# Rotary query stores, one gating piece and one cumulative sum moved to other places in a two-branch attention block

## The chip, the core and the metric

The kernel runs on one core of one Trainium2 chip. The core has five engines that work at the same time: TensorE (PE, matrix products into PSUM), VectorE (DVE), ScalarE (ACT), GpSimd (POOL) and SyncE (SP, which here only issues DMA transfers; the 16 DMA engines of the core move the data). The metric is the device time of one execution in microseconds (us), smaller being better; several executions are timed and their median is taken.

## The reference

The program is one layer of a decoder block: two attention branches side by side, latent attention with a rotary part (MLA, called branch 0 in the kernel) and attention with a forget gate (FoX, branch 1), 16 heads each, 512 real positions after 16 leading ones, width 1024, everything in float32. Cut to what matters:

```python
u = rmsnorm(h, pre_norm_g)
(cq, ckv, k_pe_raw, z_mla, fq, fk, fv, f_logit, z_fox, gate_a, gate_b) = split(u @ w_in)
q = rmsnorm(cq) @ w_uq                  # 16 heads of 64 + 32 (the 32 are rotary)
kv = rmsnorm(ckv) @ w_ukv               # 16 heads of 64 keys + 64 values
k_pe = rope(k_pe_raw, pos);  q_m = [q_nope, rope(q_pe, pos)];  k_m = [k_nope, k_pe]
o_mla = softmax(causal(q_m k_m^T * scale)) v_mla
cum = cumsum(log_sigmoid(f_logit + fox_forget_b))
o_fox = softmax(causal(fq fk^T * scale + cum[t] - cum[s])) fv
y_mla = (o_mla * silu(z_mla)) @ w_br_mla;   y_fox = (o_fox * silu(z_fox)) @ w_br_fox
mixed = (sigmoid(gate_a) * y_mla + sigmoid(gate_b) * y_fox) @ w_out
out = (h + rmsnorm(mixed, post_norm_g))[n_meta:]
```

## The kernel before

**Precision.** Each float32 factor of a product is split into a high part (rounded to the format that PE multiplies fast) and a low part (the rest), and a product is three matmuls: high x high, high x low, low x high. So each weight tile needs, after its load from HBM (`wraw`), a cast on ACT (`wh`, L127) and a subtraction on POOL (`wl`, L102) before PE can use it; the third matmul of each group of three is the first to read `wl`. Three `wraw`, `wh` and `wl` buffers go round.

**Units and fills.** The work of PE is cut into units: `fq`, `fk`, `v` (FoX queries, keys, values of a pair of heads), `mq`, `mk`, `v` (the same of MLA), `z` (the inputs of the silu, one tile of each branch), `pg` (the two gates) and `ppe` (the rotary queries of eight heads). A unit is a list of steps; a step is three matmuls over one block of 128 of the inner dimension, and the first step of a unit asks for its weights and starts the loads of the next three units. `unit`, `weights`, `wsplit` and `run` (which calls a list of steps) do this.

**Stages.** After a first part (norms, the latent projections, the first FoX queries and keys) come 16 stages, one for each pair of heads and branch, FoX and MLA by turns: stage 0 is FoX pair 0, stage 1 is MLA pair 0, stage 2 FoX pair 1, and so on. A stage is: `s0`, the scores of query blocks 0 to 2 (`st` on PE, three bank pairs of 144 + 272 and 400 columns); the value products `ov` of the stage before (`late`, `va`); `s1`, the scores of block 3; and then a fill, the units that the next stage needs, with the gates spread over some stages. Each run of scores is masked on DVE with the row extreme (`sf`, L761), exponentiated on ACT (L769), normalised and split on ACT and DVE (`pn`, L796 and L797) and transposed by eight DMA transpositions on SP (`pt<-pn`, L802). The values are transposed in the same way (`vp<-vh`, L700). `ov` needs both. The score tiles have four PSUM banks, so `s1` can begin only when DVE has read the first banks of `s0`; the units share three PSUM banks (`accp`).

**The order.** PE's order is written out by hand (a manual schedule: PE runs what the program text lists, in that order). The other engines are ordered by a scheduler that goes through the program by readiness and priority; three things tie it: `tc.high_priority`, `tc.issue_after(ins)` (what is written in the block is queued behind `ins`, if it is on the same engine) and `tc.keep_in_program_order` (queued behind what was written last on that engine). `written[0] = True` makes the helper `dma` (L90) do the last for every transfer. `behind` is a list of instructions behind which `wsplit` queues its ACT cast. Each engine then runs its own list strictly in order, so an instruction that waits holds all that follows on that engine. In the built program, transfers take one of eight completion semaphores in turn, whichever engine issues them, and the issuing engine waits until the transfer that had that semaphore before has landed.

**The places that the change touches.**

- `hl_done` (L232): the evacuation of queries and keys, a copy on ACT (L241, kept in `halved`) and the low part on DVE (L242). The keys come in two halves of 272 and 256 columns.
- L504 to L528: the first FoX queries and keys (`qk`), between them the log forget gates: `Abs`, `Exp`, `Ln` on ACT, L513 and the running sum `tensor_tensor_scan` (L514) on DVE, then `ch` (L519 on ACT, L521 on DVE), which goes out by DMA to `CT` and `c_dram`. `run(qk[7:])` holds all steps of the first keys.
- `pe_unit` (L593): the rotary queries. `rest` (L631) turns them on POOL and puts the result into `gT0` and `gT1`; those of pair 0 go to `QP` directly (L645), those of pairs 1 to 7 go by `store` (L647) to `qpe_dram` in HBM, four transfers of 192 KB, and are read back as `QP<-qpe_dram` one pair at a time, first for stage 3.
- `first` (L846): the rotary unit, the first FoX values, and the first four of the eight steps of gate unit `pg00`. The other four (`begun`) open the fill of stage 0.
- the stage loop (L880). In stage 0, `s0` and `s1` run back to back, then `fill[:5]` (four gating steps and one `z` step), the transposition of the FoX values, the `QP` transfers, both normalisations, and the rest of the fill: `z` of FoX, `mq`, `z` of MLA with `mk` and `v` in between. After it the four stores are written with `nc.scalar.dma_start`, so they are issued by ACT's queue, the first two behind the copy of `mq`, the other two behind the second copy of `mk`.

## Time and profile before

| | us |
|---|---|
| median of three timed executions (614.07 to 617.99) | 615.04 |
| the profiled execution | 616.33 |
| its span, from the first to the last instruction on the core | 614.5 |
| what lies around the span | 1.83 |
| PE busy | 600.5 (98%) |
| ACT, DVE, POOL busy | 329.9, 311.5, 264.1 |

The mean granted PE clock was 0.996 of full speed. The profile has one page of totals (busy time of each engine, the span in 40 slices, the DMA queues, the chain of waits that ended last, the costliest groups of instructions) and views into the trace: a timeline of an engine in a window (start, duration, engine, line, operation, what it writes and reads, and in brackets the idle time ahead of it and what ended it), the chain of waits in order of time, and tables of windows. In the tables of windows a row is the window, its length, the busy time of PE, PEld (weight loads), DVE, ACT and POOL with the number of instructions, the granted PE clock, the mean share of the 16 DMA engines and GB/s. SPq and ACTq are the queues from which SP and ACT issue transfers; the duration of such a row is the issuing, not the transfer. Matmuls overlap, so the time that one costs is the distance to the start of the next.

### The profile page before, as it was taken

Reading aid. Unit: us, or ns where it says so; the run is one execution under the profiler, and the core shown is the slowest. Engines: PE = TensorE matmul, PEld = TensorE weight load, DVE = VectorE, ACT = ScalarE, POOL = GpSimd, SP = SyncE. Lnnn points to the kernel's source line nnn. Section 1 sums busy time; section 2 is a strip of 40 time slices with the busy share of each in tenths; the row PEclk is TensorE's granted clock in tenths of the full one; section 3 lists DMA queues with packets and bytes.
Section 4 is the critical chain, followed back from the end, with each engine's and each line's share of the span. In section 5 each row is a group of like instructions: output and inputs, shape, how many; then the busy total and the mean of one; then the engine's idle time right before and its main releaser. Section 6 shows DMA issues by size and latency. Waiting matters only on the chain.

```text
span 614.5 us, 11031 instructions
## 1 busy us (share of the span) xinstructions
PE 600.5 (98%) x3821; PEld 508.9 (83%) x3821; DVE 311.5 (51%) x925; ACT 329.9 (54%) x758; POOL 264.1 (43%) x266
## 2 busy tenths in 40 slices
PE   7999989999999999999999999999999999999996
PEld 6888768889889889888898898878888888888885
DVE  4946637665775765675656657717222022024034
ACT  7846727765774775675667657737222232232321
POOL 4317506453437544353533534452544444444610
PEclk9999989999999999999999999999999999999999
DMA  9434487979688687997688786771523333224602
GB/s 299 102 81 127 94 173 134 226 169 206 125 178 177 153 192 161 188 185 186 145 144 179 171 176 151 175 159 36 157 84 101 103 102 97 89 91 126 251 35 102
DMA packets 223704, 89.59 MB, mean 146 GB/s; under 512 B 141772, under 2 KB 216916, under 8 KB 223648
## 3 DMA queue, kind: packets, MB, share of 16 engines
q1 hardware_dynamic: 223240, 88.09, 60.6%
q10 hardware_dynamic: 408, 0.79, 0.5%
q8 instruction: 30, 0.49, 0.3%
q14 instruction: 26, 0.21, 0.1%
HBM read 54.43 MB, written 4.00 MB: 95 GB/s over the span
## 4 chain that ended last, share of the span: by engine, by line
PE 85%; ACT 4%; DVE 4%; issue 3%; DMA 2%; POOL 1%; SPq 0%; ACTq 0%; DVEq 0%; POOLq 0%
PE py L96 14%; PE z L96 14%; PE pg L96 14%; PE po L96 7%; PE fk L96 7%; PE v L96 7%; PE fq L96 6%; PE st L96 6%; PE ov L96 4%; DVE sf L761 2%; PE psm L96 2%; PE mq L96 2%; DMA pt<-pn 1%; ACT uTh L373 1%; PE mk L96 1%
## 5 line engine op out<-in xcount | busy, mean ns | idle before, releaser
L102 POOL TENSOR_TENSOR wl<-wraw,wh 128x1024 fp32r<-128x1024 f32 (+1 forms) x90 | 208.0, 2315 | 208.4 <-ACT wh L127 202.3
L127 ACT CAST wh<-wraw 128x1024 fp32r<-128x1024 f32 (+1 forms) x90 | 89.9, 1003 | 163.6 <-issue 46.8
L769 ACT ACTIVATE sf<-sf,nb 128x144 f32<-128x144 f32 (+3 forms) x128 | 72.1, 565 | 13.8 <-DVE nb L761 13.8
L797 DVE SCALAR_TENSOR_TENSOR pn<-sf,ri,pn 128x128 f16<-128x128 f32 (+3 forms) x128 | 68.7, 575 | 13.2 <-ACT pn L796 13.1
L796 ACT ACTIVATE pn<-sf,ri 128x128 f16<-128x128 f32 (+3 forms) x128 | 61.5, 551 | 19.9 <-ACT sf L769 17.9
L957 DVE SCALAR_TENSOR_TENSOR tb<-th,py 128x512 f32<-128x512 f32 x16 | 11.0, 688 | 101.9 <-PE py L96 101.9
L96 PE MATMUL st<-hlk,hlq 64*128 64x272 f32 (+3 forms) x480 | 50.9, 310 | 1.2 <-DVE nb L761 0.6
L96 PE MATMUL z<-uTh,wh 128*128 128x512 f32 x128 | 50.8, 397 | 0.0
L761 DVE CUSTOM_DVE_ANT_0 sf<-st,maskt 128x272 f32<-128x272 f32 (+2 forms) x128 | 48.4, 435 | 3.8 <-PE st L96 2.9
L96 PE MATMUL pg<-uTh,wh 128*128 128x512 f32 x128 | 50.2, 392 | 0.0
L96 PE MATMUL z<-uTh,wl 128*128 128x512 f32 x128 | 50.0, 391 | 0.0
L96 PE MATMUL z<-uTl,wh 128*128 128x512 f32 x128 | 49.9, 390 | 0.0
L96 PE MATMUL pg<-uTl,wh 128*128 128x512 f32 x128 | 49.8, 389 | 0.0
L96 PE MATMUL pg<-uTh,wl 128*128 128x512 f32 x128 | 49.8, 389 | 0.0
L96 PE MATMUL py<-gh,wh 128*128 128x512 f32 x128 | 49.8, 389 | 0.0
L96 PE MATMUL py<-gl,wh 128*128 128x512 f32 x128 | 49.8, 389 | 0.0
L96 PE MATMUL py<-gh,wl 128*128 128x512 f32 x128 | 49.8, 389 | 0.0
L783 POOL TENSOR_TENSOR mt<-sf,ri 128x96 f32<-128x96 f32 (+1 forms) x32 | 9.5, 295 | 83.1 <-DVE ri L778 71.7
L96 PEld LDWEIGHTS st<-hlk,hlq 64*128 64x128 f32 x480 | 36.9, 185 | 8.9 <-DVE nb L761 3.4
L96 PE MATMUL ov<-pt,vp 128*64 128x256 f16 (+4 forms) x416 | 35.1, 317 | 2.7 <-DMA qpe_dram<-gT 2.7
L96 PE MATMUL v<-uTh,wh 128*128 128x256 f32 (+1 forms) x128 | 36.7, 287 | 0.6 <-DVE hlk L102 0.4
L96 PEld LDWEIGHTS <-vp 128*64 128x64 f16 (+1 forms) x416 | 22.9, 113 | 16.6 <-issue 5.3
(191 smaller groups left out, 1416.5 us busy)
## 6 DMA issues: line engine op xcount, KB each, us to landing
wraw<-in_w_in_dram SPq DMA_DIRECT2D x56, 512.0 KB, 4.7
wraw<-in_w_br_fox_dram SPq DMA_DIRECT2D x8, 512.0 KB, 3.5
wraw<-in_w_br_mla_dram SPq DMA_DIRECT2D x8, 512.0 KB, 3.8
wraw<-in_w_out_dram SPq DMA_DIRECT2D x8, 512.0 KB
pt<-pn SPq DMA_TRANSPOSE x128, 2.6
xr<-in_x_dram SPq DMA_DIRECT2D x4, 512.0 KB
out_dram<-yo SPq DMA_DIRECT2D x8, 256.0 KB, 2.0
QP<-qpe_dram SPq DMA_DIRECT2D x7, 256.0 KB, 2.8
```

Of the source, the lines that this page charges most:

```text
L96: nc.tensor.matmul(*a, **k)
L102: return eng.tensor_tensor(out=lo, in0=src, in1=f32(hi), op=ALU.subtract)
L127: nc.scalar.copy(wh[:, :n], raw[:, :n])
L373: pin(nc.scalar.activation(hi, src, AF.Copy, scale=gk))
L761: nc.vector.tensor_tensor_reduce(out=sf_of(h, b)[:, c0 : c0 + w], in0=ps[h][:, o : o + w], in1=maskt[:, m0 : m0 + w], scale=-scale, scalar ...
L769: exps[g] = nc.scalar.activation(sf, sf, AF.Exp, bias=sums["nb"][:, h, b : b + 1], scale=-1.0, accum_out=sums["su"][:, h, b : b + 1]).ins
L783: nc.gpsimd.tensor_tensor(out=mt, in0=src, in1=ri.unsqueeze(3).broadcast_to([128, 2, nb_, META]), op=ALU.mult)
L796: nc.scalar.activation(hi, sf, AF.Copy, scale=rib)
L797: nc.vector.scalar_tensor_tensor(out=lo, in0=sf, scalar=rib, in1=hi, op0=ALU.mult, op1=ALU.subtract)
L957: nc.vector.scalar_tensor_tensor(out=tb[br], in0=ths[i, br], scalar=1.0, in1=py, op0=ALU.add, op1=ALU.mult)
```

## The change

Three edits, with no change to what is computed, and with the same instructions and transfers in number:

- **The stores.** The four stores of the rotary queries are no longer written at the end of stage 0 with ACT as the issuing engine. They are written in stage 1, after its `s1` and ahead of its fill, whose first step is the transposition of the MLA values (`vp<-vh`, "second values"). SP issues them, and each is queued behind what was written last on SP.
- **The gating piece.** In stage 0, three of the four remaining steps of `pg00` (nine matmuls of 512 columns) run between `s0` and `s1` instead of after `s1`. The other stages keep their order.
- **The first keys.** The running sum on DVE is now queued behind the low part of the second half of the first keys. The ACT cast of the weights of `pg00` is queued behind the copy of that half.

```diff
-    behind, through, first_t, exps, halved = [], [], [], [], {}
+    behind, through, first_t, exps, halved, lowered = [], [], [], [], {}, {}
...
-                split_lo(nc.vector, hl[:, 1, o : o + w_], ps, hl[:, 0, o : o + w_])
+                lowered[key, i] = split_lo(nc.vector, hl[:, 1, o : o + w_], ps, hl[:, 0, o : o + w_]).ins
...
-        nc.vector.tensor_tensor_scan(out=fa[:, 0], data0=fa[:, 1], data1=fa[:, 2], initial=0.0, op0=ALU.add,
-                                     op1=ALU.add)
         run(qk[7:])
+        with tc.issue_after(lowered[("k", 1, 0), 1]):
+            nc.vector.tensor_tensor_scan(out=fa[:, 0], data0=fa[:, 1], data1=fa[:, 2], initial=0.0, op0=ALU.add,
+                                         op1=ALU.add)
...
-            def store(x, a, b, start=None):
+            def store(x, a, b):
                 for i in range(2):
-                    dma(qpe_dram[8 * g + a : 8 * g + b, i, x], results(x)[16 * a : 16 * b, i], start)
+                    dma(qpe_dram[8 * g + a : 8 * g + b, i, x], results(x)[16 * a : 16 * b, i])
...
-        run(first[len(pe0) :])
+        run(first[len(pe0) : -4])
+        behind[:] = [halved[("k", 1, 0), 1]]
+        run(first[-4:])
+        behind.clear()
...
-            for fn in [s0] + late + [s1]:
+            fill = fills[si]
+            for fn in [s0] + late:
                 fn()
-
-            fill = fills[si]
             if si == 0:
-
-                run(fill[:5])
+                run(fill[:3])
+            s1()
+
+            if si == 0:
+
+                run(fill[3:5])
                 run(vts[1, 0] + pe_rest)
                 n0()
                 n1()
                 first_t.extend(through)
                 run(fill[5:])
-                written[0] = False
-                for x in range(2):
-                    with tc.issue_after((halved[("q", 0, 0), 0], halved[("k", 0, 0), 1])[x]):
-                        store0(x, 2, 8, nc.scalar.dma_start)
-                written[0] = True
             else:
-                run(fill[:1])
-                run(fill[1:5])
+                if si == 1:
+
+                    written[0] = True
+                    for x in range(2):
+                        store0(x, 2, 8)
+                    written[0] = False
+                run(fill[:5])
```

## The prediction, made before the changed kernel was run

> **What bounds the kernel now.** The page came first: PE is busy for 600.5 of 614.5 us, so the time is PE's work and the few places where PE stands still or is slow. The table of windows says where those are.

> ```profile
> 82.00:94.00 12.00, 8.85 (x79) 6.35 (x78) 4.00 (x18) 5.33 (x16) 2.59 (x2) 0.86 0.86 174
> 94.00:200.00 106.00, 105.80 (x806) 92.32 (x807) 69.85 (x221) 68.17 (x162) 52.44 (x67) 1.00 0.83 173
> ```

> From 94 us on PE hardly stops. Between 82 and 94 us, where stage 1 begins, 3.15 us are idle and the clock was lowered (0.86 in the mean). The timeline of PE for this stretch, and for stage 3, which is the same MLA stage one pair later:

> ```profile
> 82.27 0.56 PE L96 MATMUL st<-hlk,hlq 64*128 64x144 f32 x6
> ...
> 84.56 0.40 PE L96 MATMUL ov<-pt,vp 80*64 80x512 f16 x1
> 87.62 3.61 PE L96 MATMUL ov<-pt,vp 80*64 80x512 f16 x25 [2.66 <-DMA qpe_dram<-gT]
> 91.43 0.39 PE L96 MATMUL st<-hlk,hlq 64*128 64x272 f32 x1 [0.20 <-DVE nb L761]
> ...
> 93.79 0.50 PE L96 MATMUL fq<-uTh,wh 128*128 128x512 f32 x1
> ```
> ```profile
> 130.56 0.56 PE L96 MATMUL st<-hlk,hlq 64*128 64x144 f32 x6
> ...
> 132.86 2.04 PE L96 MATMUL ov<-pt,vp 80*64 80x512 f16 x26
> ...
> 136.68 0.50 PE L96 MATMUL fq<-uTh,wh 128*128 128x512 f32 x1
> ```

> From the first score to the first `fq` stage 3 takes 136.68 - 130.56 = 6.12 us, stage 1 takes 93.79 - 82.27 = 11.52 us, with the same instructions. The 5.40 us between them are three things: `ov` waits from 84.96 to 87.62; its other 25 matmuls take 3.61 us where stage 3 needs 2.04 for 26; and the second score run then waits for DVE (`nb`). What `ov` waits for is seen in the chain of waits, on ACT's queue and on SP's:

> ```profile
> 78.41 9.12 DMA pt<-pn
> ...
> 87.61 0.71 ACTq L90
> ```
> ```profile
> 75.66 2.10 ACTq L90 DMA_DIRECT2D qpe_dram<-gT  x2
> ...
> 80.67 7.65 ACTq L90 DMA_DIRECT2D qpe_dram<-gT  x2
> 88.37 0.29 ACT L687 ACTIVATE vh<-v,vsc 128x32 f16<-128x32 f32 x1 [9.11 <-DMA pt<-pn]
> ```
> ```profile
> 68.39 13.32 SPq L90 DMA_TRANSPOSE pt<-pn  x8
> 81.77 2.32 SPq L90 DMA_DIRECT2D wraw<-in_w_in_dram  x2
> 84.18 2.62 SPq L90 DMA_DIRECT2D CT<-c_dram  x2
> 90.82 1.27 SPq L90 DMA_TRANSPOSE vp<-vh  x1
> ```
> ```profile
> pt<-pn SPq DMA_TRANSPOSE x128, 2.6
> ```

> The last of stage 0's eight transpositions is issued at 78.41 and lands at 87.53, 9.12 us later, against a median of 2.6. In just that time the stores of the rotary queries are in flight. ACT issues the fourth store at 87.61, as soon as that transposition has landed: it holds the completion semaphore that the store is to have. So ACT stands from 80.67 to 88.32 inside its pair of stores, and the value copies (`vh`), the silu and all exponentials behind it are late; DVE, in order behind ACT, reads the scores late, which is the third part of the 5.40 us.

> [...]

> ```profile
> 88.00:90.00 2.00, 2.00 (x14) 1.25 (x12) 0.82 (x3) 1.63 (x5) 0.00 (x0) 0.50 0.61 171
> ```

> After an idle time of 2.66 us the granted clock was 0.50. [...]

> **The change part by part.** *The stores.* Removed from ACT: two pairs of issues (2.10 and 7.65 us) and the wait inside the second. Added to SP: four issues. They are queued behind the last weight load written in stage 0, so behind all eight transpositions and the two loads. Without stores among them I let the eighth transposition be issued at 78.41 as now and land after the median, at 81.0, which is 3.5 us before `ov` asks for it at 84.56. ACT then runs `vh` and the silu when their inputs are there (the last `z` matmul ends close to 82.27), and DVE reaches the scores in the manner of stage 3. So stage 1 becomes stage 3: minus 5.40 us. What is late next is nothing that a row shows: the cast of `fq`'s weights follows the silu on ACT, which ends near 83.5; with 1.04 on ACT and 2.40 on POOL (rows below) they are there at about 87, and `fq` would begin at 82.27 + 6.12 = 88.39. What the stores cost on SP: the pair on ACT that did not wait took 2.10, so four take about 4.2; with the transpositions through at about 79.7, two loads (2.32), four stores (4.2), the two `CT` loads (2.62) and the `vp` transposition (1.27) SP is free at about 90.1. Queued behind them are the next weight load and the transpositions of stage 1:

> ```profile
> 96.13 2.48 SPq L90 DMA_TRANSPOSE pt<-pn  x2
> ...
> 107.51 3.57 SPq L90 DMA_TRANSPOSE pt<-pn  x2
> ```
> ```profile
> 111.62 1.88 PE st L96 x24
> 113.50 1.97 PE ov L96 x26
> 115.47 1.17 PE st L96 x16
> ```

> Those are wanted 5.7 us sooner than now, at 90.4. The cover is thus 0.3 us on SP, and behind it some 1.6 us more: the last of them is issued half way through the second row, at about 109.3, lands with the median at 111.9, and its `ov` begins at 113.50 (the chain of waits in stage 2). I take nothing for it. The stored data are read by SP for stage 3 only, after 111 us. Bounds of this part: 5.40 if all of it goes, 1.0 if the transposition still lands at 87.53 (second rival).

> *The gating piece.* Rows for stage 0, PE first, then ACT and POOL; the unhindered lengths of the same two runs stand in the chain of stage 2 above:

> ```profile
> 61.22 0.56 PE L96 MATMUL st<-hlk,hlq 64*128 64x144 f32 x6
> ...
> 65.56 0.50 PE L96 MATMUL pg<-uTh,wh 128*128 128x512 f32 x1
> ...
> 67.73 0.39 PE L96 MATMUL pg<-uTh,wh 128*128 128x512 f32 x1
> ...
> 75.69 0.40 PE L96 MATMUL z<-uTh,wl 128*128 128x512 f32 x1
> ```
> ```profile
> 62.93 0.42 ACT L769 ACTIVATE sf<-sf,nb 128x144 f32<-128x144 f32 x1 [2.05 <-DVE nb L761]
> ...
> 71.74 1.04 ACT L127 CAST wh<-wraw 128x1024 fp32r<-128x1024 f32 x1
> ```
> ```profile
> 72.86 2.40 POOL L102 TENSOR_TENSOR wl<-wraw,wh 128x1024 fp32r<-128x1024 f32 x1 [3.62 <-ACT wh L127]
> ```

> The two score runs take 65.56 - 61.22 = 4.34 us and need 1.88 + 1.17 = 3.05. Nine gating matmuls (67.73 - 65.56 = 2.17 us) between them cover DVE's reading, so PE is through 1.29 us sooner. But the next thing is near: the second `z` unit needs `wl` at 75.69, and POOL has it at 72.86 + 2.40 = 75.26, only 0.43 us before. Its cast at 71.74 stands on ACT at the end of 8.8 us without a hole (62.93 to 71.74: exponentials, the gate, `pn`). This length does not change, so if ACT stays filled `wl` is there at 75.26 again and PE, early, waits: nothing gained. If ACT has a hole, because the scores of block 3 now end at 61.22 + 1.88 + 2.17 + 1.17 = 66.44 instead of 65.56, `wl` comes 0.88 later and PE loses 0.88 - 0.43 = 0.45. If the scheduler puts the cast ahead of some `pn`, up to 1.29 are gained. I take 0, the value of the rows as they stand, with -0.45 and +1.29 for the range.

> *The first keys.*

> ```profile
> 51.55 0.40 PE L96 MATMUL ppe<-cTh,wl 128*128 128x512 f32 x1
> 52.37 0.39 PE L96 MATMUL v<-uTh,wh 128*128 128x272 f32 x1 [0.42 <-DVE hlk L102]
> ...
> 55.44 0.35 PE L96 MATMUL v<-uTh,wh 128*128 128x256 f32 x1
> ```
> ```profile
> 52.84 1.90 DVE L521 SCALAR_TENSOR_TENSOR ch<-fa,ch 16x528 fp32r<-16x528 f32 x1
> 54.67 1.87 DVE L628 TENSOR_TENSOR pt<-ppe,pt 128x512 f32<-128x512 f32 x3
> ```

> PE's step from 51.55 to 52.37 is 0.82 us, where the nine gating matmuls of the same width took 2.17 / 9 = 0.24 each: 0.58 us of waiting for the key's low part to free a bank. With the low part ahead of the running sum (and the copy ahead of a cast as long as the 1.04 above) this wait goes. The cast for `pg00`, now queued behind the copy, and its subtraction on POOL start some 0.4 us later; PE reaches `pg00` only after the second half of `v`, which begins at 55.44. That second half, early, asks at 54.86 for the bank that the first of the three products at 54.67 frees, at 54.67 + 0.62 = 55.3. If DVE keeps `ch` (1.90) ahead of that product, the wait is back there and nothing is gained; if the product passes, because the sum and so `ch` are ready later, 0.58 stays. Which one no row shows, so I take the middle, 0.3. The later `ch` is covered: it ends at 54.74, and the first scores, which read it by way of `CT`, begin 6.5 us later.

> **Sum.** 5.40 + 0 + 0.3 = 5.7 us. The profiled execution would go from 616.33 to 610.6; it lay 1.29 above the median of the runs, so the median goes from 615.04 to 609.3. Its own range: 5.40 with -0.45 to 5.40 + 0.58 + 0.45 gives 5.0 to 6.4 us, 608.6 to 610.1.

> **The rivals.** *First, more than forecast:* the cast for the second `z` moves ahead on ACT, so that the gating piece counts in full: 5.40 + 1.29 + 0.3 = 7.0 us, 608.0. For it: a cast that the scheduler finds ready takes any hole on ACT, and the gate unit that frees its buffer ends sooner. Against: the hole is under 1 us, and `pn` stands ahead in program order.

> *Second, the wait at `ov` stays:* the transposition lands at 87.53 for another reason than the stores. ACT is no longer held then, so only the wait for DVE after `ov` goes: `ov` ends at 87.62 + 3.61 = 91.2, the second run needs at the half clock about 1.6, `fq` begins at 92.8 instead of 93.79: 1.0 us, 614.0. Against it: 9.12 against a median of 2.6, and the releaser that the profile names for `ov` is a store. [...]

> *Third, slower:* SP takes over ACT's wait. If each pair of stores holds SP for 7.65 us, the four take 15.3 instead of 4.2, SP is free at 101.2 instead of 90.1, the transpositions of stage 1 are held up by 101.2 - 90.4 = 10.8 us, and the `ov` of stage 2, with 1.6 us of margin, waits 10.8 - 1.6 = 9.2 us and runs at half clock (1.6 more): 10.8 - 5.7 = 5.1 slower, 620.1. It decides from the point at which the four hold SP for some 10 us (4.2 + 0.3 + 1.6 are covered, 5.7 - 1.6 eat the gain). Against it: the stores' semaphores belong on SP to transfers issued before them on the same queue, which have landed by then.

> *Fourth, no effect:* the scheduler issues the stores among the transpositions after all: about 615. The pinned order speaks against it.

> **How the numbers follow.** Forecast 0.59, first rival 0.23, second 0.10, third 0.04, fourth 0.04. One per cent is 6.15 us, about what a measurement of this kernel can tell from no change. Faster by more than that (below 608.9): the first rival and a quarter or more of the forecast, 0.40. Slower by more (above 621.2): a longer hold in the third rival, 0.02. Within: 0.58. The range holds the first rival and the forecast with 0.8 on the low side for scatter of runs, and on the high side 2.2 for a wait at `ov` that goes only in part: 607.2 to 612.3; what is left out is rivals two to four, 0.18.

> **What would show it.** Right: in the timeline of PE from the first MLA score to the first `fq` about 6.1 us, no `ov` row with a wait, a granted clock of 1.00 from 82 to 94 us; no ACTq row for `qpe_dram`; the eighth transposition landing within 3 us. The gating piece: no wait for `nb` in the first scores, and then the start of the second `z` and what ended the idle time ahead of it (POOL `wl`: nothing gained). The keys: `v` directly behind `ppe`, and the start of its second half. Wrong: a wait of `ov` in stage 1 or 2 for a transposition, SP rows for `qpe_dram` of more than 2 us each, or any new PE gap after 94 us.

## The result, and the profile after

The changed kernel takes 611.79 us in the median of seven executions (610.42 to 613.73), the kernel before 615.04 (seven in the same series, 614.07 to 617.99): ratio 0.994, interval 0.9916 to 0.9964. It is faster by 3.25 us where 5.7 were forecast; the median lies inside the range that was given (607.2 to 612.3), 0.5 us from its upper end, and the gain is under one per cent. The profiled execution took 613.73 us, with a span of 611.9.

The table of windows, for the stretch that had 3.15 us of idle PE and a clock of 0.86 (here 2 us later, see below):

```profile
84.00:96.00 12.00, 12.00 (x106) 9.66 (x105) 9.72 (x33) 10.74 (x28) 7.71 (x8) 1.00 0.92 194
```

PE is busy for all 12 us, at full clock. Its timeline, with the rows that begin the parts of the sum:

```profile
50.96 0.40 PE L96 MATMUL ppe<-cTh,wh 128*128 128x512 f32 x1
...
53.77 0.29 PE L96 MATMUL v<-uTh,wh 128*128 128x272 f32 x1
...
62.44 0.56 PE L96 MATMUL st<-hlk,hlq 64*128 64x144 f32 x6
...
77.60 0.50 PE L96 MATMUL z<-uTh,wl 128*128 128x512 f32 x1 [1.59 <-POOL wl L102]
...
84.31 0.56 PE L96 MATMUL st<-hlk,hlq 64*128 64x144 f32 x6
...
86.60 2.04 PE L96 MATMUL ov<-pt,vp 80*64 80x512 f16 x26
...
89.99 0.50 PE L96 MATMUL fq<-uTh,wh 128*128 128x512 f32 x1
...
109.33 0.40 PE L96 MATMUL ov<-pt,vp 80*64 80x512 f16 x1
109.93 2.03 PE L96 MATMUL ov<-pt,vp 80*64 80x512 f16 x25 [0.20 <-DMA pt<-pn]
...
260.51 2.01 PE L96 MATMUL ov<-pt,vp 80*64 80x512 f16 x25 [0.93 <-issue]
```

The steps from row to row, beside those of the kernel before:

| from, to | before | after | gained |
|---|---|---|---|
| first `ppe`, first score (keys) | 12.24 | 11.48 | 0.76 |
| first score, third matmul of the second `z` (gating piece) | 14.47 | 15.16 | -0.69 |
| from there to the first MLA score | 6.58 | 6.71 | -0.13 |
| first MLA score, first `fq` (stores) | 11.52 | 5.68 | 5.84 |
| first `fq`, scores behind the `ov` of stage 2 | 21.61 | 21.91 | -0.30 |
| from there to the last matmul | 493.57 | 494.48 | -0.91 |
| first `ppe` to the last matmul | 559.99 | 555.42 | 4.57 |

So 5.78 us had been won at `fq`, 5.7 were forecast, and 1.2 went again later. In the row of -0.30 PE waits 0.20 us in front of the `ov` of stage 2, for a transposition. 0.90 is lost at the row of 260.51, in the `ov` of stage 9, whose wait of 0.93 us has no releaser in the profile. SP's row of the transpositions of the stage before it, the last six of eight, is

```profile
250.81 8.04 SPq L90 DMA_TRANSPOSE pt<-pn  x6
```

The last of them lands at 260.42 by the semaphore updates in the trace (which give the time of each landing), 0.09 us before `ov` goes on. In the second profile of the changed kernel (below) the wait there is 0.32 us, and it ends 0.09 us behind the same landing, at 259.42. So this too is a wait for SP's transpositions: counted from the first `ppe`, SP was through with them 4.61 us sooner than in the kernel before (207.89 against 212.50), and PE, 5.45 us sooner up to there, fell back to 4.55.

The rest of the way from 4.57 to the 2.6 us between the two spans lies ahead of `ppe`, which starts 1.98 us later after the change than before, behind the same instructions. The windows of the first 20 us, of the kernel before and of the changed one:

```profile
0.00:20.00 20.00, 16.31 (x83) 13.43 (x83) 11.20 (x34) 15.28 (x38) 6.64 (x13) 1.00 0.84 269
```
```profile
0.00:20.00 20.00, 16.05 (x65) 13.85 (x66) 10.39 (x32) 14.00 (x35) 6.61 (x13) 0.91 0.85 267
```

The granted clock was 0.91 there instead of 1.00. All thirteen profiles of this study fall into two groups: clock 1.00 and `ppe` at 48.98 to 49.60 us (nine), or 0.91 and `ppe` at 50.26 to 50.96 (four). The nine hold the kernel before and versions with and without the change's parts, the four the changed kernel (twice) and two of its versions. In each of the four the clock record has one stretch of 3.41 us at 0.50 that begins between 9.2 and 10.9 us (here 10.93 to 14.35, which makes the 0.91), and in none of the nine is there one so early. The change itself does not bring it, since versions that contain it stand in both groups. What is compared from here on is counted from the first `ppe`.

ACT around the gating piece, after the change:

```profile
67.92 2.51 ACT L797 ACTIVATE pn<-sf,ri 128x128 f16<-128x128 f32 x6 [0.62 <-DVE ri L779]
...
72.82 1.34 ACT L797 ACTIVATE pn<-sf,ri 128x512 f16<-128x512 f32 x2 [0.47 <-DVE ri L779]
74.06 1.04 ACT L127 CAST wh<-wraw 128x1024 fp32r<-128x1024 f32 x1
```

The scores of block 3 come later, so the scheduler has put six `pn` ahead of their exponentials. ACT now waits twice for a reciprocal (0.62 and 0.47 us). Counted from the first score, the cast stands 1.10 us later than before (11.62 against 10.52; the two raw times, 74.06 and 71.74, hold the later start of this execution as well), and POOL has `wl` 1.07 us later, at 77.55. And SP, which issues the stores:

```profile
69.65 11.09 SPq L90 DMA_TRANSPOSE pt<-pn  x8
80.78 1.20 SPq L90 DMA_DIRECT2D wraw<-in_w_in_dram  x2
82.03 5.07 SPq L90 DMA_DIRECT2D qpe_dram<-gT  x4
87.20 0.74 SPq L90 DMA_DIRECT2D CT<-c_dram  x2
88.03 3.09 SPq L90 DMA_TRANSPOSE vp<-vh  x1
...
92.03 3.07 SPq L90 DMA_TRANSPOSE pt<-pn  x2
...
104.26 3.57 SPq L90 DMA_TRANSPOSE pt<-pn  x2
```

From 69.65 on SP has hardly a gap. Its sixteenth transposition (eight of stage 0, eight of stage 1) is issued by 104.26 + 3.57 = 107.83 us, and `ov` goes on 2.10 us behind that.

### The profile page after: what moved, and what is told of

Read it like the earlier page. It is cut to its first block, busy times and chain, and to the rows that moved or that the text cites. A ratio compares the mean times of both kernels' runs of the same rounds, so it can differ in the third digit from the quotient of the medians.

```text
span 611.9 us, 11030 instructions
## 1 busy us (share of the span) xinstructions
PE 599.1 (98%) x3821; PEld 509.6 (83%) x3821; DVE 311.8 (51%) x925; ACT 329.7 (54%) x758; POOL 263.8 (43%) x266
## 4 chain that ended last, share of the span: by engine, by line
PE 89%; ACT 3%; DVE 3%; issue 2%; DMA 1%; POOL 0%; SPq 0%; DVEq 0%; ACTq 0%
PE py L96 14%; PE pg L96 14%; PE z L96 14%; PE v L96 9%; PE fk L96 7%; PE fq L96 7%; PE po L96 7%; PE st L96 6%; PE ov L96 4%; PE psm L96 3%; DVE sf L762 2%; PE mq L96 2%; PE mk L96 1%; PE ppe L96 1%; DMA ht<-in_x_dram 1%
## 5 line engine op out<-in xcount | busy, mean ns | idle before, releaser
L102 POOL TENSOR_TENSOR wl<-wraw,wh 128x1024 fp32r<-128x1024 f32 (+1 forms) x90 | 207.8, 2312 | 204.0 <-ACT wh L127 202.1
L127 ACT CAST wh<-wraw 128x1024 fp32r<-128x1024 f32 (+1 forms) x90 | 89.9, 1003 | 164.9 <-issue 50.5
L96 PE MATMUL z<-uTh,wl 128*128 128x512 f32 x128 | 50.2, 392 | 1.6 <-POOL wl L102 1.6
L96 PE MATMUL z<-uTh,wh 128*128 128x512 f32 x128 | 50.8, 397 | 0.0
L96 PE MATMUL pg<-uTh,wh 128*128 128x512 f32 x128 | 50.3, 393 | 0.0
L96 PE MATMUL z<-uTl,wh 128*128 128x512 f32 x128 | 49.9, 390 | 0.0
L96 PE MATMUL pg<-uTl,wh 128*128 128x512 f32 x128 | 49.8, 389 | 0.0
L96 PE MATMUL pg<-uTh,wl 128*128 128x512 f32 x128 | 49.8, 389 | 0.0
L96 PE MATMUL py<-gh,wh 128*128 128x512 f32 x128 | 49.8, 389 | 0.0
L96 PE MATMUL py<-gl,wh 128*128 128x512 f32 x128 | 49.8, 389 | 0.0
L96 PE MATMUL py<-gh,wl 128*128 128x512 f32 x128 | 49.8, 389 | 0.0
L96 PE MATMUL st<-hlk,hlq 64*128 64x272 f32 (+3 forms) x480 | 49.5, 308 | 0.2
L96 PEld LDWEIGHTS st<-hlk,hlq 64*128 64x128 f32 x480 | 36.2, 185 | 7.1 <-ACT wh L127 2.5
L96 PE MATMUL v<-uTh,wh 128*128 128x256 f32 (+1 forms) x128 | 36.5, 285 | 0.0
L96 PE MATMUL fk<-uTl,wh 128*128 128x256 f32 (+1 forms) x128 | 36.4, 285 | 0.0
L96 PE MATMUL v<-uTl,wh 128*128 128x256 f32 (+1 forms) x128 | 36.4, 285 | 0.0
```

The lines of the kernel that those rows point to most:

```text
L96: nc.tensor.matmul(*a, **k)
L102: return eng.tensor_tensor(out=lo, in0=src, in1=f32(hi), op=ALU.subtract)
L127: nc.scalar.copy(wh[:, :n], raw[:, :n])
```

## The experiments

Each ratio is to the kernel before, timed beside it on the same chip. The table gathers what the later sections draw on, in us counted from the first `ppe` of each profile.

| kernel | `ov` of stage 1 ends | SP is through with the 16th transposition | PE idle ahead of the `ov` of stage 2 | end of the last matmul | ratio (interval) |
|---|---|---|---|---|---|
| before | 42.25 | 62.10 | none | 559.99 | 1 |
| changed | 37.68 | 56.87 | 0.20 | 555.42 | 0.994 (0.992 to 0.996) |
| changed, again | 37.66 | 57.05 | 0.41 | 555.12 | one run |
| stores alone | 37.63 | 57.16 | 0.39 | 555.27 | 0.995 (0.993 to 0.997) |
| without the gating piece | 36.89 | 57.82 | 1.82 | 556.28 | 0.993 (0.991 to 0.995) |
| early cast | 35.85 | 57.87 | 3.03 | 557.43 | 0.993 (0.991 to 0.995) |
| early cast, `CT` by ACT | 35.87 | 57.59 | 2.77 | 555.74 | 0.995 (0.993 to 0.997) |
| early cast, loads by ACT | 35.87 | 55.94 | none | 558.92 | 0.999 (0.997 to 1.000) |
| gating piece alone | 38.36 | 59.45 | 0.23 | 557.42 | one run |
| stores by POOL | 44.94 | 60.97 | none | 561.88 | one run |
| eight heads | 37.69 | 56.44 | none | 554.48 | one run |
| eight heads, timed | 37.69 | 57.16 | 0.40 | 554.98 | 0.990 (0.987 to 0.994) |
| early cast, `CT` by ACT, eight heads | 35.84 | 57.05 | 2.14 | 556.38 | 0.991 (0.988 to 0.995) |

The intervals of all but one overlap; what tells the versions apart is the profile.

**Stores alone.** The kernel before with the stores' edit only.

```diff
-                with tc.issue_after((halved[("q", 0, 0), 0], halved[("k", 0, 0), 1])[x]):
-                    store0(x, 2, 8, nc.scalar.dma_start)
...
+                if si == 1:
+                    written[0] = True
+                    for x in range(2):
+                        store0(x, 2, 8)
+                    written[0] = False
...
```

> Only the stores' edit: SP issues the four stores behind the eight transpositions, the gating piece and the keys' scan stay as before. Theory: the whole gain of the change is made here. From the first MLA score to the first fq the profile shows 5.7 to 6.1 us instead of 11.52, no wait of the stage's ov for a transposition, clock 1.00 there, and the fourth store ends on SP late enough that the ov of the next stage waits about 0.6 us for its transposition. Time 0.990 to 0.993 of the kernel before, about the same as the whole change (0.994). Rival: the whole change needs the gating piece to fill what the stores leave; then this run gives less than 3 us (above 0.995).

The stage took 88.37 - 82.69 = 5.68 us and `ov` did not wait; the `ov` of stage 2 waited 0.39. The count from `ppe` to the end is that of the whole change within 0.15 us: by the profiles the theory holds, and the other two edits add nothing to the end. The ratio, 0.995, is above the 0.990 to 0.993 that were expected.

**The change without its gating piece.** `run(fill[:3])` between `s0` and `s1` is taken out, `run(fill[:5])` follows `s1` as before.

> The whole change without its gating piece: the two first score runs stand back to back again. Theory: the piece cost 0.69 us between the first score and the third matmul of the second z (15.16 against 14.47), so this kernel is about 0.7 us faster than the whole change (ratio to the kernel before about 0.993), the second z waits less than 0.5 us for POOL's wl, and ACT has no hole of 0.62 and 0.47 us in the first stage's exponentials. Rival: the 0.69 us are lost anyway, because the second score run waits for the DVE pass as before (1.29 us); then the time is the same as the whole change's, and the profile shows the wait for nb.

At the `ov` of stage 1 it was 0.79 us ahead of the changed kernel, as expected. But its timeline of PE at the `ov` of stage 2 reads:

```profile
109.53 0.38 PE L96 MATMUL ov<-pt,vp 80*64 80x512 f16 x1 [1.43 <-DMA pt<-pn]
110.29 2.04 PE L96 MATMUL ov<-pt,vp 80*64 80x512 f16 x25 [0.39 <-DMA pt<-pn]
```

The lead is lost in these two waits, and the count ends 0.86 us above that of the changed kernel. Neither case had said so.

**The early cast.** The changed kernel with the cast of the second `z` put ahead of the exponentials of block 3.

```diff
+        with tc.high_priority(offset=ahead_by[0]) if ahead_by[0] else nullcontext():
+            with tc.issue_after(behind[0]) if behind else nullcontext():
+                nc.scalar.copy(wh[:, :n], raw[:, :n])
+            split_lo(nc.gpsimd, wl[:, :n], raw[:, :n], wh[:, :n])
...
+                ahead_by[0] = 200
+                run(fill[14:15])
+                ahead_by[0] = 0
...
```

> The whole change, with the cast of the second z unit's weights put ahead of the fourth block of exponentials on ACT (nothing else is moved). Theory: the 1.59 us that the third matmul of the second z waits for POOL's wl are set by the cast's place on ACT (74.06 us in the changed kernel, 71.74 before); with the cast some 2.3 us sooner the wait is gone and the kernel is 1.0 to 1.6 us faster than the whole change (ratio to the kernel before 0.991 to 0.993). Rival: the two last pn and their transpositions come about 1.3 us later for it, and the ov of this stage or the next waits for a transposition instead; then the wait of 1.59 us is gone but the time is the whole change's.

The wait of 1.59 us was gone and the `ov` of stage 1 ended 1.83 us sooner than in the changed kernel. The rival came in, at stage 2 and dearer than it said:

```profile
108.82 0.38 PE L96 MATMUL ov<-pt,vp 80*64 80x512 f16 x1 [2.61 <-DMA pt<-pn]
109.61 3.54 PE L96 MATMUL ov<-pt,vp 80*64 80x512 f16 x25 [0.42 <-DMA pt<-pn]
```

3.03 us of waiting, and behind it the half clock (0.50 granted from 110 to 113 us, and 3.54 instead of 2.04 us). By the profile the version is 2.0 us slower than the changed kernel; the ratio, 0.993, does not show that, so a part of it may be this one execution's (the 1.50 us of the half clock first of all; see the last section).

**Stores by POOL.** In the kernel before, `nc.gpsimd.dma_start` for `nc.scalar.dma_start`, behind the second `z`'s `wl`.

> The kernel before, with its four stores issued by POOL behind the second z's wl, at about the time at which ACT issued its first two; ACT issues no DMA there, SP's queue is as before. Theory A, the eighth transposition landed late (9.12 us from its issue, against 2.6) because the stores' many short pieces share the DMA engines with it: then it lands as late here, the ov of this stage waits 2 to 3 us again and the stage takes 10 to 11.5 us. Theory B, it landed late because of what ACT and its queue did (its own hold, or the two hardware queues taking turns): then it lands within 3 to 4 us of its issue, no wait is left in front of ov, and the stage takes 6 to 7 us, the time some 4 to 5 us below the kernel before.

PE's timeline, and the eighth transposition in the chain of waits:

```profile
88.82 0.39 PE L96 MATMUL ov<-pt,vp 80*64 80x512 f16 x1 [3.94 <-issue]
90.38 3.80 PE L96 MATMUL ov<-pt,vp 80*64 80x512 f16 x25 [1.17 <-DMA pt<-pn]
```
```profile
84.82 5.47 DMA pt<-pn
```

Theory A, and more than it asked: with all four stores issued by 78.02 us, and no DMA on ACT, the waits at `ov` grew from 2.66 to 5.11 us, and the stage took 13.80 us. SP itself stood for 7.26 us in the issue of the seventh transposition, and the eighth, issued only at 84.82, landed 5.47 us later, at 90.29, just ahead of the second row of `ov`. The first row went on 0.09 us behind the landing of the seventh (88.73). ACT's hold is not needed for the eighth transposition to be late; the stores' traffic is enough.

**The gating piece alone.**

> The kernel before, with the gating piece alone (keys, scan and stores as before). Theory: ACT takes the order that it has in the changed kernel (two holes of about 0.5 us, the cast of the second z's weights some 1.5 to 2.5 us later), the third matmul of the second z waits 1 to 1.6 us for POOL's wl, and from the first score to there it takes 0.5 to 0.8 us longer than in the kernel before (14.47 us); the ov of stage 1 still waits for its eighth transposition, which takes up what the piece lost, so that the end, counted from ppe, is within 1 us of the kernel before. Rival: the piece is worth its 1.29 us of PE work and the second z does not wait; then this stretch takes about 13.2 us.

To the second `z` it cost 0.60 us, as expected (76.71 - 61.64 = 15.07 against 14.47). But the wait at `ov` was gone and the count fell by 2.57 us, which no case had said. ACT's rows of the stores:

```profile
75.02 2.35 ACTq L90 DMA_DIRECT2D qpe_dram<-gT  x2
79.69 0.73 ACT L241 CAST hlk<-mk 128x272 fp32r<-128x272 f32 x2 [4.32 <-PE mk L96]
82.59 2.72 ACTq L90 DMA_DIRECT2D qpe_dram<-gT  x2
```

And from the chain of waits:

```profile
80.43 4.09 DMA pt<-pn
...
84.60 0.71 ACTq L90
```

The copy of the keys behind which the third store is queued ends at 80.42, but the store goes out only at 82.59: ACT waits for the completion semaphore of the sixth transposition, which lands at 82.57. In the kernel before that copy ended at 79.26, the sixth transposition landed at 80.64, and the third store went out at 80.67. So the sixth transposition landed late in both, 6.68 and 5.28 us after its issue, beside the first two stores. What differs is the eighth. SP was through with it at 82.40 (81.71 before), so the third store now comes behind it, and it landed 4.09 us after its issue instead of 9.12; before, the third store went out 1.04 us ahead of SP's end with it, and that is what `ov` waited for (the store landed at 86.90, the transposition at 87.53; here the third store lands at 88.23, when `ov` is done). It has the effect of the edit of the stores, by accident and in part: 4.15 of the 5.84 us in the stage. ACT still stood until 85.31 inside its pair of stores, and the second score run of the stage waited 0.67 and 0.20 us for DVE behind it.

**Four loads by ACT.** The early cast, with SP relieved of four 64 KB loads.

```diff
-                          + [kv[:, i, 2 * pr : 2 * pr + 2, :] for i in range(2)], wrap)
+                          + [kv[:, i, 2 * pr : 2 * pr + 2, :] for i in range(2)], wrap, pr == 1)
...
+                if by:
+                    other[:] = [nc.scalar.dma_start, exps[1]]
```

> The kernel with the early cast, with four small loads (w_uq and w_ukv, 64 KB each) taken from SP's queue, where they stand between the transpositions of stage 1's probabilities, and issued by ACT behind its last exponentials of that stage (ACT has a hole of 1.93 us there). Theory A, the ov of stage 2 waits because SP issues too slowly behind the stores: SP is 2.1 us lighter (four loads by 0.53), its sixteenth transposition is issued some 2 us sooner and ov, which started its second part 2.1 us behind that in all four runs so far, comes 2 us sooner; the waits of 2.61 and 0.42 us in front of ov shrink to under 1.2 us, and the time falls by 2 to 3.5 us against the early cast alone (ratio to the kernel before 0.987 to 0.990). Theory B, SP is not slow but waits for landings (it holds the next transposition until a DMA eight places earlier has landed): the rows of SP grow longer by what was taken out, ov waits as before within 0.7 us, and the time is that of the early cast (0.993).

ACT's timeline:

```profile
93.00 3.52 ACTq L90 DMA_DIRECT2D wraw<-in_w_uq_dram  x2
...
98.98 1.00 ACTq L90 DMA_DIRECT2D wraw<-in_w_ukv_dram  x2
100.11 1.33 ACT L802 ACTIVATE pn<-sf,ri 128x512 f16<-128x512 f32 x2 [7.09 <-DMA pt<-pn]
```

On SP theory A is right: it is through 1.93 us sooner (55.94 against 57.87). That `ov` does not wait says little, because PE came to it late: the loads held ACT from 93.00 to 99.98, as the stores had done in the kernel before, what stands behind them on ACT was delayed, and PE stood in the middle of `v`:

```profile
102.93 0.58 PE L96 MATMUL v<-uTh,wh 128*128 128x256 f32 x1 [4.99 <-DVE hlq L102]
```

The version loses to the early cast (0.999 against 0.993, where 0.987 to 0.990 were expected).

**`CT` by ACT.** The early cast, with `nc.scalar.dma_start` for the two `CT` loads of pair 1, queued behind the second copy of the first MLA keys.

> The kernel with the early cast, with the two CT loads (4 KB each, 0.75 us on SP) issued by ACT in its hole in front of the first vh of stage 1, instead of by SP in front of the transposition of vh. Theory A (SP's issue time is what counts): the transposition of vh and all behind it come 0.75 us sooner, and the wait of 2.61 us in front of stage 2's ov shrinks by as much. Theory B (SP's row vp<-vh of 3.52 us, against 1.27 in the kernel before, is a wait for the first 512 KB load behind the eighth transposition to land, some 9 us after its issue): the row starts sooner and is longer by the same 0.75 us, it ends as late as before (9.0 to 9.5 us behind the start of that load's row, plus 1.3), and neither ov nor the time moves.

The row of the `vp` transposition on SP, of this kernel and of the early cast, and a row of ACT of the early cast:

```profile
86.03 4.00 SPq L90 DMA_TRANSPOSE vp<-vh  x1
```
```profile
86.99 3.52 SPq L90 DMA_TRANSPOSE vp<-vh  x1
```
```profile
86.85 1.04 ACT L128 CAST wh<-wraw 128x1024 fp32r<-128x1024 f32 x1
```

The row grew by 0.48 of the 0.75 us: most of SP's time in it is waiting, not issuing (1.27 us were enough in the kernel before). Counted from `ppe` it ended 1.15 us sooner, but only 0.28 of that was left when SP was through with the sixteenth transposition. The wait is not for the 512 KB load, as theory B had it: its cast ran on ACT at 86.85 without a wait, over 2 us before the transposition went through (86.99 + 3.52 - 1.27 = 89.24). That leaves the stores themselves as the candidate. The count from `ppe` to the end is 1.69 us lower than that of the early cast; 1.50 of it is the half clock, which this execution did not have (2.04 us for the 25 `ov`, against 3.54).

**Stores over eight heads.** The changed kernel with `store0(x, 0, 8)` for `store0(x, 2, 8)`: heads 0 and 1 are stored too, and nobody reads them.

> The changed kernel, with each of the four stores over all eight heads of the group instead of six (8x16x512 instead of 6x16x512; a third more bytes, the rest as in the changed kernel). Theory A, a store is spread over as many of the 16 DMA engines as its outermost dimension has entries: behind the two 512 KB loads the DMA engines show a mean busy share of 0.50 instead of 0.37 to 0.42, some 205 GB/s instead of 154, and this stretch in front of the transposition of vh is as long as before (3 to 4 us), so that the transposition lands as late as in the changed kernel, within 0.5 us, counted from the first store's row. Theory B, the stores are bound by something that all engines share: the share stays at 0.4 at about 154 GB/s, the stretch is a third longer, and the row of vp<-vh ends 1 to 1.5 us later.

The DMA engines from 83 to 91 us in 40 steps of 0.2 us (busy share in tenths, and the rate), of the changed kernel and of this one:

```profile
DMA  9999999999999743333435252333444533434699
GB/s 325 315 351 333 346 338 353 340 338 292 323 335 405 223 156 143 154 154 154 154 123 113 61 102 82 133 154 143 164 123 133 92 92 106 170 146 172 198 234 244
```
```profile
DMA  9999999999988555555554545555555556899985
GB/s 330 346 297 338 338 338 320 330 343 353 346 289 305 205 205 205 205 205 205 195 215 184 225 184 205 205 205 195 215 195 205 205 200 234 266 303 262 174 141 100
```

After the loads (some 340 GB/s, all engines) the rate keeps coming back to 154 GB/s at 0.3 to 0.4 in the one, and holds 205 at 0.5 in the other: divided by six and by eight that is 25.7 and 25.6 GB/s. So, by an estimate from these rates and shares, a store of 6x16x512 ran on six of the 16 DMA engines (6/16 = 0.38) and one of 8x16x512 on eight (8/16 = 0.50); no run shows single engines. Theory A is right on the share; that the `vp` transposition went through 1.06 us sooner, counted from the first store's row (8.03 against 9.09), it had not said, and why is open.

> The changed kernel with stores over eight heads, again, with the timing that the one look lacked. Theory: it repeats its 554.5 us from ppe to the end within 0.5 us, without a wait in front of the ov of stage 2, which is 0.6 to 0.9 us under the two profiles of the changed kernel; the ratio to the kernel before is 0.991 to 0.993, too near to the changed kernel's 0.994 (0.9916 to 0.9964) for the times to tell the two apart. Rival: the transposition of vh landed sooner by chance; then ppe to the end is 555.1 to 555.5 us again and the wait of 0.2 to 0.7 us in front of that ov is back.

The `vp` transposition was early again (8.23), but three transpositions behind it took 5.40 us instead of 4.60, `ov` waited 0.40 and the count came out 0.5 us higher (554.98): something of both cases. Both profiles lie below both of the changed kernel, by 0.14 to 0.94 us. This is the best version found, and its time is not separable from the changed kernel's.

**The changed kernel again.**

> The changed kernel as it is, once more. Theory: what differs from execution to execution lies ahead of the first rotary matmul (ppe), which stood at 48.98 to 50.96 us in the profiles so far, and from there on the program repeats itself: 555.4 us from ppe to the last matmul, within 0.8 us, with ppe anywhere between 48.9 and 51. Rival: the late ppe of the changed kernel (50.96) belongs to the change; then ppe is at 50.5 to 51.5 again.

555.12 us from `ppe` to the end, against 555.42. `ppe` was late again (50.26), just under the rival's 50.5, so this run alone does not refute it; the early cast, its version with loads on ACT and eight heads do, which have the whole change in them and `ppe` at 49.04 to 49.60.

**All together.** Early cast, `CT` by ACT, eight heads.

> What the runs so far point to, put together: the changed kernel with the early cast (no wait of the second z for wl, 1.8 us sooner at the ov of stage 1), the two CT loads on ACT, and stores over eight heads (the transposition of vh about 1 us sooner). Theory: the sixteenth transposition sets the time at the ov of stage 2, and only what makes SP's run up to it shorter counts: with act_ct's row and one us less, SP has issued it 56.5 us after ppe (56.4 to 57.9 in the variants so far), ov is 2.1 us behind that, its first wait is 1 to 1.5 us instead of 2.34, and from ppe to the end it takes 554.0 to 554.8 us, against 555.74 (act_ct), 555.4 and 555.1 (the changed kernel) and 554.5 (eight heads alone). Rival: with the stores' share of the DMA engines grown, the first transpositions of stage 1 are slower by what vh's gained, and the time is act_ct's within 0.3 us. Either way the ratio to the kernel before is 0.990 to 0.994.

SP was through at 57.05, half a microsecond later than expected, and the wait was 1.82 + 0.32 us. Most of the miss (556.38 where 554.0 to 554.8 were expected) is the clock. PE's `ov` of stage 2 and the windows from there, and the window at the same place in the version without eight heads, which had waited longer (2.34 + 0.43):

```profile
107.66 0.49 PE L96 MATMUL ov<-pt,vp 80*64 80x512 f16 x1 [1.82 <-DMA pt<-pn]
108.47 3.37 PE L96 MATMUL ov<-pt,vp 80*64 80x512 f16 x25 [0.32 <-DMA pt<-pn]
```
```profile
106.00:108.00 2.00, 0.34 (x1) 0.11 (x1) 1.50 (x8) 1.68 (x4) 0.55 (x1) 0.95 1.23 279
108.00:111.00 3.00, 2.68 (x16) 1.57 (x17) 0.36 (x2) 2.49 (x11) 1.82 (x2) 0.50 1.05 312
111.00:112.00 1.00, 1.00 (x16) 0.88 (x13) 0.12 (x1) 1.00 (x4) 0.93 (x4) 0.89 0.98 267
```
```profile
110.00:112.00 2.00, 1.96 (x25) 1.50 (x25) 0.00 (x1) 1.97 (x8) 1.37 (x1) 1.00 1.12 339
```

The half clock cost 3.37 - 2.04 = 1.33 us here and nothing there.

## Why the prediction came out as it did

The range held and the change stayed under one per cent, and the mechanism of the main part was the forecast one; the gain was overstated. That the median fell inside the range is in part luck: the high side of the range was made for a wait at the `ov` of stage 1 that goes only in part, and that wait went whole. What took up the gain was in other terms, some of them with errors that cancel.

- **Stores, 5.40.** Right: 5.84 in the stage, no wait at `ov`, clock 1.00, no row of ACT for the stores. The 0.44 above the forecast lie in the second score run, which took 1.42 us up to `fq` where stage 3 had needed 1.85. That traffic beside the transposition was the cause is shown twice, by POOL's stores (the wait grows) and by the gating piece alone (the third store behind the transposition, and the wait goes). The second and third rivals fall: the four stores held SP for 5.07 us where 4.2 were estimated, not 15.3.
- **Gating piece, 0.** Wrong by 0.69 and beyond the bound of -0.45. The step that failed is "This length does not change", with one hole of 0.88 at most as the bad case: the scheduler reordered `pn` and exponentials, which made two holes of 1.09 us together, and the cast slipped by 1.10 us where 0.43 were covered.
- **First keys, 0.3.** Low by 0.46, and beyond the 0.58 that was given as the most: the product passed `ch` on DVE, the case that no row had shown, and `v` follows `ppe` without a wait (0.58 gained). The other 0.18 lie between there and the first score and are not followed further.
- **"I take nothing for it."** This is the term that was missing, and the last line of the prediction had named its sign, a wait of `ov` in stage 2. The margin of 1.6 us at the `ov` of stage 2 was counted from the median landing of a transposition issued half way through the row; the runs show `ov` 2.1 us behind the end of that row, 62.10 + 2.1 us after `ppe` in the kernel before, where `ov` was at 113.43 - 48.98 = 64.45. So the margin was about 0.3. The sixteenth transposition came 5.23 us sooner, `ov` began 6.08 us sooner, and the scores behind it came 5.48 sooner: what was won beyond about 5.5 was given back there. The same holds in the versions: where the `ov` of stage 1 ends between 35.8 and 37.7, SP, unless the four small loads are taken from it, is through between 56.4 and 57.9, whatever was won ahead. The step of the table that holds this place lost 0.30 us. The larger loss, 0.90 in this profile, is the same kind of wait in the `ov` of stage 9, which the prediction did not look at; in the second profile of the changed kernel the two cost 0.50 and 0.29.
- **The median.** 4.57 and 4.87 us from `ppe` on, against 3.25 between the medians (2.2 to 5.2 by the interval). The rest lies most likely in the start ahead of `ppe`, which moves by 2 us from execution to execution; the executions that were only timed do not show it.

## What to carry to other kernels

A transfer that delays one that is wanted sooner can be moved behind it (here the eighth transposition then landed 2.90 us after its issue instead of 9.12); but look up who is next in the new queue, and count its margin from the end of the whole row of issues (here 2.1 us to `ov`), not from a median landing. A gain is worth what is left of it at the next point where another chain (here SP with its transpositions) catches up: once a version is paced there, gains upstream turn into waits (3.03 us in the early cast), and a wait may cost the clock on top (0.50 behind the 1.82 us of all together, which cost 1.33 us). Such a point can come more than once: here in stage 2 and in stage 9. Before a small load or store is given to another engine, ask what it has to wait for: here it held its engine for as long (ACT from 80.67 to 88.32 us in the second pair of stores of the kernel before, from 93.00 to 99.98 in the four loads).

## What the runs showed of the hardware

```profile
104.39:107.80 3.41, 1.59 (x21) 1.23 (x19) 2.68 (x13) 1.48 (x4) 0.35 (x1) 1.00 1.19 277
107.80:111.21 3.41, 3.09 (x18) 1.75 (x19) 0.36 (x2) 2.90 (x11) 2.23 (x2) 0.50 1.03 303
```
```profile
104.89:108.30 3.41, 2.00 (x26) 1.62 (x24) 2.71 (x13) 0.80 (x2) 0.00 (x0) 1.00 1.04 239
108.30:111.71 3.41, 2.05 (x23) 1.41 (x24) 0.24 (x2) 3.41 (x12) 2.36 (x1) 1.00 1.13 302
```

The wait of 1.82 us lay whole in one window; that of 2.34, with the 0.43 behind it, was split by the edge at 108.30 into 1.41 and 1.36. Over all thirteen profiles, among the windows at full clock that end ahead of the last matmul, each one in which PE stood idle for 1.67 us or more was followed by one at 0.50, and none with 1.59 or less was. So what counted here is whether about half of a window (1.67 of 3.41 us) was idle. The edges lie elsewhere in each execution, so one version can show a half clock and a like one not. The four late starts fit this too: PE was idle for 1.67 to 1.89 us in the first window of their record, and for at most 1.48 in that of the other nine.
